# Half steps and a new list of steps in the attention stage of a hybrid decoder trunk

## The chip, the cores and the metric

The kernel runs on one core of one Trainium2 chip. The metric is device time in microseconds of one execution. TensorE (PE) multiplies, VectorE (DVE) and ScalarE (ACT) work on tiles in SBUF and on PSUM banks, GpSimd (POOL) does little here, and SyncE (SP) issues all loads.

## The reference

Two layers; each normalizes `x` (256 x 1024), projects it to 3100 columns, runs three groups of heads side by side, and ends with an MLP:

```python
for layer in range(DEPTH):                       # DEPTH = 2
    h = _rmsnorm(x, norm1_g[layer])
    proj = h @ w_in[layer]                       # 1024 x 3100
    o_a = _hgrn2(...)   # gated linear recurrence, 4 heads, state 64 x 64
    o_b = _nsa(...)     # 8 heads, 2 key groups: compressed + selected + window attention
    o_c = _fox(...)     # forgetting attention, 4 heads
    x = x + concat(o_a, o_b, o_c) @ w_o[layer]
    h2 = _rmsnorm(x, norm2_g[layer])
    x = x + square(relu(h2 @ w_up[layer])) @ w_down[layer]     # 1024 -> 4096 -> 1024
```

## The kernel before

All of it is one program without loops at run time. Weights come as 512 KB tiles of 128 x 1024 (`load`, tag `raw`, four slots). `load_split` (L223, L224) makes a high part `whi` on ACT and the rest `wlo` on DVE, and `mm3` (L229 to L231) multiplies three times, high by high, high by low, low by high. So every weight tile costs one long instruction on ACT, one on DVE and a run of products.

A layer has an attention stage and an MLP stage. In the attention stage, `proj_tok` and `proj_feat` make one of the projected chunks: "ag", "af", "ai", "aq" for the recurrence, "cmp" for the compressed keys and values, "kk", "q0", "q1" and "vg" for the sparse attention, "ck", "cq" and "cv" for the forgetting attention. A chunk is 48 products into one of two `acc` banks. "cv", "kk" and "q0" come first (`FIRST`).

The chains behind the chunks are these. The recurrence runs through seven levels `a_level` ("t0" to "t6"): a product of `Kc` and `Qbd` (L470), a masked copy of it (L479), and updates of `Qbd` and `Kc` on DVE (L485, L487) that the next level's product needs; `a_out` closes it. Keys and queries are normalized per head (`head_norm`), turned by four transposes (`head_transposes`, L560) and split again (`b_keys` L584, L585; `b_query` L595, L596; `c_query`, `c_keys`). The compressed keys take 16 small products per quarter (`b_compress`, "w0" to "w3", L613), whose weights `raw1` are used unsplit and hold `raw` slots till then, then `b_compressed` ("kc"): transposes, a GELU on DVE and ACT, a product that reads `hidT` (L640), a normalization, a transpose (L652) and the split into `KC` (L658, L659). `b_cmp_branch` ("cb0", "cb1") makes the compressed scores with `KC` (L772), a softmax, and transposes (L799). `head_b` ("b0" to "b7") and `head_c` ("c0" to "c3") make scores, softmax (L751 on DVE, L161 on ACT), scaling (L757 on ACT, L759 on DVE), transposes (L836, L841; L884) and a copy out of PSUM (L838, L843; L887); `pv_b` ("pb") and `pv_c` ("pc") multiply by the values (L850, L858; L895). "forget" prepares the decay. `wo_step` ("wo0" to "wo3") adds one weight tile each to the first column half of the output projection; the second half follows the list.

`ORDER` lists these steps; "+name" starts a chunk's projection, "name" does what follows it. The loop at the end of the stage calls them in that sequence. The sequence gives preference; the build then sorts the instructions of each engine and assigns slots, so the order on an engine need not be that of the list. PSUM has two `acc`, two `sc`, two `tr`, one `pa` and one `pv` bank. The list before:

```python
ORDER = ("+ag", "+af", "+cmp", "+aq", "kk", "af", "aq", "cmp", "t0", "+vg", "q0", "t1", "t2", "t3", "vg", "b2",
         "b1", "w0", "t4", "w1", "cv", "+ai", "w2", "w3", "ai", "t5", "kc", "b0", "+q1", "q1", "cb0", "t6", "b3",
         "cb1", "pb0", "forget", "a_out", "+ck", "+cq", "ck", "pb1", "cq", "b4", "b5", "b6", "c0", "pb2", "b7",
         "pb3", "c1", "wo0", "pc0", "wo1", "c3", "wo2", "c2", "pc1", "wo3")
```

Of the kernel before, what the change touches and what calls it, by code (L numbers as in the profile page):

```python
# [24 lines left out]
DH = 64  # L25
EPS = 1e-6
# [26 lines left out]
FIRST = ("cv", "kk", "q0")  # L53
ORDER = ("+ag", "+af", "+cmp", "+aq", "kk", "af", "aq", "cmp", "t0", "+vg", "q0", "t1", "t2", "t3", "vg", "b2",
# [3 lines left out]
WO_LAST = (0, 1, 2, 3)  # L58
# [77 lines left out]
def tile_block(ctx: ExitStack, tc: tile.TileContext, x_in, win, wo, wup, wdn, w1, vec, cst, out, dbg=None):  # L136
# [39 lines left out]
    def bank(tag):  # L176
        return T([P, 512], F32, tag, BANKS[tag], pp)
# [163 lines left out]
    for L in range(DEPTH):  # L341
# [149 lines left out]

        def a_out():
# [12 lines left out]
            V.tensor_copy(sd, psd[:, :8])  # L505
            po = bank("pa")
# [17 lines left out]
            V.tensor_mul(oA, oA, GA)  # L524
            ps = bank("pa")
# [50 lines left out]

        def b_keys(ps):

            ptr = head_transposes(head_norm(ps, 2, 4, 2, EPS, tabs["k"]), swap=(0,))
            for g in range(2):  # L580
# [7 lines left out]

        def b_query(c, ps):
            ptr = head_transposes(head_norm(ps, 2, 4, 1, DH * EPS, tabs["q"]))  # L590
            for a in range(2):
# [23 lines left out]

        def b_compressed():
            pre = pre_[0]
# [19 lines left out]
            V.reciprocal(u, u)  # L637
            V.tensor_mul(hidT[:, :, :, 0:NCMP], hx, u.rearrange("p (w g n) -> p w g n", w=2, g=2))
            pk = bank("sc")
            PE.matmul(pk[0:64, 0:64], hidT[:, 0].rearrange("p g n -> p (g n)"), vt[:, V_W2:V_W2 + 64], start=True, stop=True)  # L640
# [8 lines left out]
            V.tensor_sub(VC[64:80, :, 64:128], pvv, VC[0:16, :, 64:128].bitcast(F32))  # L649
            kcn = head_norm(pk[0:64, 0:64], 1, 1, 1.0 / DH, EPS, tbc, 64)  # L650
            pkt = bank("tr")
# [41 lines left out]

        def c_query(ps):
            ptr = head_transposes(head_norm(ps, 2, 4, 1, DH * EPS))
            for a in range(2):
# [5 lines left out]

        def c_keys(ps):
            ptr = head_transposes(head_norm(ps, 2, 4, 2, EPS))
            ckv = CK.rearrange("p (i a) t -> p a i t", a=2)
# [57 lines left out]
        def b_cmp_branch(g):  # L763

            ps = bank("sc")
            for j in range(4):
                hd = g * 4 + j
# [24 lines left out]
            A.activation(PCS[:, :, 64:80], pc, AF.Copy)  # L792
            V.tensor_sub(PCS[:, :, 32:48], pc, PCS[:, :, 0:16].bitcast(F32))
            pct = T([96, 4, S], F32R, "PCT", 2)
            for i in range(2):
# [13 lines left out]

        PT = {}  # L810

        def head_b(g, j):
# [18 lines left out]
            for i, (o, n) in enumerate(((0, P), (P, P), (256, 256), (512, 256))):  # L831
                scale(pt_[:, o:o + n], r[:, i:i + 1], i in SCALE_ACT)

            ps0 = bank("tr")
# [30 lines left out]
        def head_c(hd):  # L865
# [14 lines left out]
            for t, (o, n) in enumerate(((0, P), (P, 256))):  # L880
                scale(pt_[:, o:o + n], r[:, t:t + 1], t + 4 in SCALE_ACT)
            ps0 = bank("tr")
            for i in range(3):
# [60 lines left out]
        def wo_step(i):  # L944
# [8 lines left out]
            "ag": (proj_tok, None), "ai": (proj_tok, a_values), "af": (proj_feat, a_sigmoids), "aq": (proj_feat, a_query),  # L953
            "cmp": (proj_feat, b_cmp), "kk": (proj_tok, b_keys), "q0": (proj_tok, lambda ps: b_query(0, ps)),
            "q1": (proj_tok, lambda ps: b_query(1, ps)), "cq": (proj_tok, c_query), "ck": (proj_tok, c_keys),
            "cv": (proj_tok, c_values), "vg": (proj_vals, b_values),
        }
        step = {
            "t": a_level, "w": b_compress, "kc": b_compressed, "a_out": a_out,
            "cb": b_cmp_branch, "b": lambda i: head_b(i // 4, i % 4), "pb": lambda i: pv_b(i // 2, i % 2),  # L960
            "c": head_c, "pc": pv_c, "forget": c_forget, "wo": wo_step,
        }
# [164 lines left out]
```

## Time and profile before

| | us |
|---|---|
| median of three runs | 697.14 (696.44 to 698.15) |
| profiled execution, device time | 699.06 |
| its span, first to last instruction | 697.3 |
| attention stage of the first layer | from 29.5 to about 160.5 |
| attention stage of the second layer | from 371.8 to about 502.5 |
| TensorE busy | 675.9 |
| VectorE busy | 451.6 |
| ScalarE busy | 398.0 |

The stages overlap at their ends, so their bounds are rounded. A matmul's end is modelled, and products follow each other faster than one lasts; TensorE's idle time is therefore counted only when a gap outlasts the modelled end. PEclk 1.00 is the full clock, 2.4 GHz, and 0.50 is 1.2 GHz. In a timeline row the bracket gives the idle time of the engine ahead of the instruction and what ended it.

### The profile page before, as it was taken

How to read it: one execution, taken by the hardware profiler on the slowest of the kernel's cores; microseconds unless marked ns; L12 is line 12 of the kernel's file. 1: busy time of each engine (PE TensorE's matmuls, PEld its weight loads, DVE VectorE, ACT ScalarE, POOL GpSimd, SP SyncE). 2: the span in 40 equal slices, each digit the busy share in tenths (PEclk: the TensorE clock that was granted, in tenths of full speed). 3: DMA queues.
4: the chain of work that ended last, by engine and by line, in shares of the span. 5: the costliest groups of instructions: out<-in, count | busy, mean ns of one | idle time of the engine just before them, and what ended most of it. 6: DMA issues, size and time to landing. Idle time of an engine off the chain costs nothing.

```text
span 697.3 us, 11902 instructions
## 1 busy us (share of the span) xinstructions
PE 675.9 (97%) x4578; PEld 602.4 (86%) x4578; DVE 451.6 (65%) x987; ACT 398.0 (57%) x761; POOL 10.9 (2%) x28
## 2 busy tenths in 40 slices
PE   6999989999999999999999999899999999999997
PEld 5998979768988998899799988786799988998896
DVE  5878788838655545654587897786567456545552
ACT  7654675887444434554457556688865445444440
POOL 3100000000100000000000000000000000000000
PEclk9999998999999999999999999999999999999999
DMA  8852561206566666666546418421266666666631
GB/s 289 265 153 73 174 189 49 73 1 211 168 203 181 181 185 183 192 182 194 153 128 213 150 31 260 133 62 31 86 190 180 184 191 196 180 185 181 185 118 61
DMA packets 31017, 108.88 MB, mean 156 GB/s; under 512 B 3568, under 2 KB 4080, under 8 KB 30960
## 3 DMA queue, kind: packets, MB, share of 16 engines
q1 hardware_dynamic: 30960, 108.11, 51.5%
q8 instruction: 36, 0.59, 0.3%
q14 instruction: 21, 0.17, 0.1%
HBM read 107.05 MB, written 1.05 MB: 155 GB/s over the span
## 4 chain that ended last, share of the span: by engine, by line
PE 82%; DVE 8%; ACT 5%; DMA 3%; issue 1%; SPq 0%; ACTq 0%
PE sc L229 9%; PE sc L230 9%; PE sc L231 9%; PE acc L229 9%; PE acc L231 8%; PE acc L230 8%; PE pv L230 3%; PE pv L231 3%; PE pv L229 3%; DMA raw<-in_win_dram 3%; PE pa L231 3%; PE pa L230 3%; PE pa L229 3%; DVE wlo L224 2%; PE pv L858 2%; PE sc L613 1%
## 5 line engine op out<-in xcount | busy, mean ns | idle before, releaser
L224 DVE TENSOR_TENSOR wlo<-raw,whi 128x1024 fp32r<-128x1024 f32 (+2 forms) x197 | 235.2, 1197 | 139.1 <-PE sc L231 67.2
L223 ACT ACTIVATE whi<-raw 128x1024 fp32r<-128x1024 f32 (+2 forms) x197 | 204.3, 1041 | 195.1 <-PE sc L230 73.3
L229 PE MATMUL sc<-kt,whi 128*128 128x256 f32 x512 | 145.1, 283 | 0.0
L231 PE MATMUL sc<-kt,wlo 128*128 128x256 f32 x512 | 144.9, 283 | 0.0
L230 PE MATMUL sc<-kt,whi 128*128 128x256 f32 x512 | 144.8, 283 | 0.0
L229 PEld LDWEIGHTS sc<-kt,whi 128*128 128x128 f32 x512 | 98.0, 191 | 1.0 <-ACT s L1015 0.3
L230 PEld LDWEIGHTS sc<-kt,whi 128*128 128x128 f32 x512 | 98.1, 192 | 0.6
L231 PEld LDWEIGHTS sc<-kt,wlo 128*128 128x128 f32 x512 | 98.1, 192 | 0.0
L229 PE MATMUL acc<-whi,kt 128*128 128x256 f32 (+2 forms) x288 | 88.9, 309 | 2.7 <-ACT whi L223 2.7
L231 PE MATMUL acc<-whi,kt 128*128 128x256 f32 (+2 forms) x288 | 88.4, 309 | 0.2
L230 PE MATMUL acc<-wlo,kt 128*128 128x256 f32 (+2 forms) x288 | 87.4, 305 | 0.0
L229 PEld LDWEIGHTS acc<-whi,kt 128*128 128x128 f32 x288 | 56.8, 197 | 5.3 <-ACT whi L223 3.3
L231 PEld LDWEIGHTS acc<-whi,kt 128*128 128x128 f32 x288 | 56.3, 196 | 3.3 <-DVE kt L239 1.1
L230 PEld LDWEIGHTS acc<-wlo,kt 128*128 128x128 f32 x288 | 56.3, 196 | 1.5 <-DVE wlo L224 0.4
L229 PE MATMUL acc<-whi,big 128*128 128x512 f32 x128 | 50.7, 396 | 0.0
L230 PE MATMUL acc<-wlo,big 128*128 128x512 f32 x128 | 50.6, 395 | 0.0
L231 PE MATMUL acc<-whi,big 128*128 128x512 f32 x128 | 50.5, 394 | 0.0
L161 ACT ACTIVATE big<-big,nmx 128x128 f32<-128x128 f32 (+1 forms) x80 | 35.6, 447 | 16.4 <-DVE nmx L751 16.3
L1016 DVE TENSOR_TENSOR s<-s 128x512 f32<-128x512 f32 x32 | 22.0, 688 | 24.1 <-ACT s L1015 24.1
L751 DVE CUSTOM_DVE_ANT_0 big<-sc,cst 128x128 f32<-128x128 f32 (+1 forms) x80 | 26.5, 349 | 8.0 <-PE sc L876 4.2
L1015 ACT ACTIVATE s<-sc 128x512 f32<-128x512 f32 x32 | 18.8, 588 | 18.7 <-PE sc L231 18.7
L231 PEld LDWEIGHTS acc<-whi,big 128*128 128x128 f32 x128 | 24.1, 188 | 5.8
(299 smaller groups left out, 1183.3 us busy)
## 6 DMA issues: line engine op xcount, KB each, us to landing
raw<-in_wup_dram SPq DMA_DIRECT2D x64, 512.0 KB, 3.6
raw<-in_wdn_dram SPq DMA_DIRECT2D x64, 512.0 KB, 3.6
raw<-in_win_dram SPq DMA_DIRECT2D x44, 512.0 KB, 4.5
raw<-in_wo_dram SPq DMA_DIRECT2D x16, 512.0 KB, 3.9
raw<-in_w_dram SPq DMA_DIRECT2D x8, 512.0 KB, 3.6
raw<-in_win_dram SPq DMA_DIRECT2D x4, 426.0 KB, 3.7
out_dram<-x SPq DMA_DIRECT2D x4, 256.0 KB, 2.0
raw<-in_win_dram SPq DMA_DIRECT2D x2, 284.0 KB, 2.7
```

Source lines behind the costliest of these rows:

```text
L161: r = A.activation(*a, **k)
L223: A.activation(hi[:, c0], raw[:, c0], AF.Copy)
L224: V.tensor_sub(lo[:, c0], raw[:, c0], hi[:, c0].bitcast(F32))
L229: PE.matmul(ps, ah, wh, start=start, stop=False)
L230: PE.matmul(ps, ah, wl, start=False, stop=False)
L231: PE.matmul(ps, al, wh, start=False, stop=stop)
L613: PE.matmul(pre_[0][64 * w:64 * w + 35, 0:P], Z[:, w].rearrange("p g m -> p (g m)")[:, j:j + 273:8], raw1[w][:, c0:c0 + P], start=(j == 0) ...
L751: V.tensor_tensor_reduce(out=dst, in0=ps, in1=mask, scale=-1.0, scalar=3.0e38, op0=ALU.add, op1=ALU.min, accum_out=nmx)
L858: PE.matmul(po[64 * e_:64 * e_ + 64, t * P:S], VS[:, t, bi * 2 + g, :], PT[g * 4 + jj * 2 + e_][t][:, bi, :], start=False, stop=False)
L1015: A.activation(rl, pu[i], AF.Relu)
L1016: V.tensor_mul(rl, rl, rl)
```

## The change

Steps are cut in two or three at the point where one engine hands to another. `head_norm` is called by "kk", "q0", "q1", "ck" and "cq", and the transposes and splits of these become steps of their own, "/kk" and so on. `head_b` ends after the scaling, and its transposes become "h0" to "h7"; `head_c` is cut in the same place into "c" and "g", `b_cmp_branch` into "cb" and "ct", `a_out` into "ao0" to "ao2", and `b_compressed` into "kc0" to "kc2". The list of steps gets a new order with the new names. No instruction is added or dropped.

```diff
-ORDER = ("+ag", "+af", "+cmp", "+aq", "kk", "af", "aq", "cmp", "t0", "+vg", "q0", "t1", "t2", "t3", "vg", "b2",
-         "b1", "w0", "t4", "w1", "cv", "+ai", "w2", "w3", "ai", "t5", "kc", "b0", "+q1", "q1", "cb0", "t6", "b3",
-         "cb1", "pb0", "forget", "a_out", "+ck", "+cq", "ck", "pb1", "cq", "b4", "b5", "b6", "c0", "pb2", "b7",
-         "pb3", "c1", "wo0", "pc0", "wo1", "c3", "wo2", "c2", "pc1", "wo3")
+ORDER = ("kk", "+ag", "+af", "q0", "af", "+aq", "/kk", "/q0", "+cmp", "cmp", "aq", "t0", "+vg", "t1", "vg", "cv",
+         "b2", "t2", "b1", "h1", "t3", "w0", "w1", "+ai", "t4", "h2", "w2", "ai", "w3", "t5", "kc0", "kc1", "kc2",
+         "b0", "+q1", "t6", "q1", "h0", "cb0", "/q1", "ct0", "forget", "b3", "pb0", "ao0", "cb1", "h3", "pb1",
+         "+ck", "ao1", "+cq", "ck", "b4", "ct1", "cq", "b5", "h4", "/ck", "b6", "ao2", "h5", "/cq", "h6", "b7",
+         "wo1", "wo0", "h7", "c0", "c1", "g0", "g1", "pb2", "pb3", "c3", "wo2", "c2", "pc0", "g3", "g2", "pc1",
+         "wo3")
...
-        def b_keys(ps):
-
-            ptr = head_transposes(head_norm(ps, 2, 4, 2, EPS, tabs["k"]), swap=(0,))
+        def b_keys(xn):
+
+            ptr = head_transposes(xn, swap=(0,))
...
             for i, (o, n) in enumerate(((0, P), (P, P), (256, 256), (512, 256))):
                 scale(pt_[:, o:o + n], r[:, i:i + 1], i in SCALE_ACT)
+            PU[hd] = pt_
+
+        def head_bt(g, j):
+            hd = g * 4 + j
+            pt_ = PU.pop(hd)
 
             ps0 = bank("tr")
...
-            "cmp": (proj_feat, b_cmp), "kk": (proj_tok, b_keys), "q0": (proj_tok, lambda ps: b_query(0, ps)),
-            "q1": (proj_tok, lambda ps: b_query(1, ps)), "cq": (proj_tok, c_query), "ck": (proj_tok, c_keys),
+            "cmp": (proj_feat, b_cmp), "kk": (proj_tok, lambda ps: head_norm(ps, 2, 4, 2, EPS, tabs["k"])),
+            "q0": (proj_tok, lambda ps: head_norm(ps, 2, 4, 1, DH * EPS, tabs["q"])),
...
+        turn = {"kk": b_keys, "q0": lambda xn: b_query(0, xn), "q1": lambda xn: b_query(1, xn), "cq": c_query, "ck": c_keys}
+        normed = {}
...
+            elif name[0] == "/":
+                turn[name[1:]](normed[name[1:]])
             elif name in chunk:
-                chunk[name][1](ready[name])
+                normed[name] = chunk[name][1](ready[name])
```

## Rows read from the trace of the kernel before

**Rows 1.** The page: the span, and TensorE's busy time, share and instructions.
```profile
span 697.3 us, 11902 instructions
PE 675.9 (97%) x4578; PEld 602.4 (86%) x4578; DVE 451.6 (65%) x987; ACT 398.0 (57%) x761; POOL 10.9 (2%) x28
```

**Rows 2.** Windows by stage: start and end, length, each engine's busy time (instructions), clock.
```profile
core 0: us, PE busy (x) PEld busy (x) DVE busy (x) ACT busy (x) POOL busy (x), PEclk, DMA share, GB/s
29.49:52.60 23.11, 23.11 (x196) 23.11 (x195) 17.79 (x40) 13.04 (x20) 0.00 (x0) 1.00 0.59 185
52.60:160.50 107.90, 102.47 (x732) 85.73 (x731) 82.16 (x283) 76.59 (x206) 0.00 (x0) 0.97 0.30 94
160.50:371.80 211.30, 211.30 (x1367) 191.67 (x1366) 124.97 (x166) 108.94 (x153) 1.77 (x5) 1.00 0.62 183
371.80:502.50 130.70, 125.12 (x929) 108.16 (x928) 101.88 (x334) 89.78 (x227) 0.00 (x0) 0.99 0.36 111
```

**Rows 3.** TensorE's waits, 29.49 to 160.50 us: total, times, longest.
```profile
PE sc L640 <- DVE hidT L638: 1.2, 1, 1.2
PE pa L470 <- DVE m L487: 1.2, 2, 0.7
PE sc L772 <- DVE KC L659: 1.1, 1, 1.1
PE tr L841 <- ACT P L838: 0.7, 1, 0.7
```

**Rows 4.** TensorE's waits, 371.80 to 502.50 us; L772 and L841 have the same rows.
```profile
PE sc L640 <- DVE hidT L638: 1.5, 1, 1.5
PE pa L470 <- DVE m L487: 0.7, 1, 0.7
```

**Rows 5.** TensorE's timeline, 55 to 62 us: start, duration, instruction, idle time ahead.
```profile
55.68 1.15 PE L470 MATMUL pa<-Qbd,m 128*128 128x128 f32 x8
56.57 0.38 PE L229 MATMUL acc<-whi,kt 128*128 128x284 f32 x1
56.79 0.29 PE L230 MATMUL acc<-wlo,kt 128*128 128x284 f32 x1
56.92 0.29 PE L231 MATMUL acc<-whi,kt 128*128 128x284 f32 x1
...
60.56 0.60 PE L560 MATMUL tr<-cst,s 128*128 128x128 f32 x4
61.83 1.14 PE L470 MATMUL pa<-Qbd,m 128*128 128x128 f32 x8 [0.67 <-DVE m L487]
```

**Rows 6.** VectorE's timeline, 56 to 67 us: splits of the keys and queries.
```profile
59.62 0.76 DVE L585 SCALAR_TENSOR_TENSOR KLB<-tr,vec,KS 64x512 fp32r<-64x512 f32 x1
...
62.68 0.74 DVE L596 SCALAR_TENSOR_TENSOR qS<-tr,vec,qS 64x512 fp32r<-64x512 f32 x1
```

**Rows 7.** TensorE's timeline, 89 to 91 us: the product that reads `hidT`.
```profile
89.14 0.28 PE L229 MATMUL acc<-whi,kt 128*128 128x256 f32 x1
90.63 0.33 PE L640 MATMUL sc<-vec,hidT 128*64 128x64 f32 x2 [1.22 <-DVE hidT L638]
```

**Rows 8.** ScalarE's timeline, 86 to 88 us.
```profile
86.40 1.06 ACT L223 ACTIVATE whi<-raw 128x1024 fp32r<-128x1024 f32 x1 [1.58 <-DMA raw<-in_win_dram]
87.36 0.24 ACT L161 ACTIVATE gu<-gu 128x60 f32<-128x60 f32 x1
```

**Rows 9.** Waits of SP's queue, whole span: total, times, longest.
```profile
SPq L213 <- PE sc L613: 41.2, 4, 17.2
```

**Rows 10.** Windows in which the granted clock is low; columns as in rows 2.
```profile
104.80:111.65 6.85, 6.67 (x29) 6.39 (x30) 4.26 (x26) 2.02 (x7) 0.00 (x0) 0.50 0.27 77
449.56:452.98 3.42, 3.42 (x16) 3.14 (x16) 2.05 (x14) 1.85 (x7) 0.00 (x0) 0.50 0.13 53
```

**Rows 11.** Groups by line, whole span: busy, mean ns, idle ahead.
```profile
L161 ACT ACTIVATE big<-big,nmx 128x128 f32<-128x128 f32 (+1 forms) x80 | 35.6, 447 | 16.4 <-DVE nmx L751 16.3
L757 ACT ACTIVATE big<-big,rr 128x128 f32<-128x128 f32 (+1 forms) x48 | 18.8, 446 | 1.1 <-DVE rr L830 0.9
```

More of the change, by code (lines that the diff above doesn't have):

```diff
@@ L490, in a_level, with a_out0 @@
                 V.tensor_mul(th[0], tv[:, :, :, 0], tv[:, :, :, 1])
-        def a_out():
+        def a_out0():
             ps = bank("pa")
@@ L505, in a_out, with a_out1 @@
             V.tensor_copy(sd, psd[:, :8])
+            aos[:] = [AO, sd]
+        aos = []
+        def a_out1():
+            AO, sd = aos
             po = bank("pa")
@@ L524, in a_out, with a_out2 @@
             V.tensor_mul(oA, oA, GA)
+            aos[:] = [oA]
+        def a_out2():
+            oA = aos[0]
             ps = bank("pa")
@@ L587, in tile_block, with b_query @@
         qS = [T([P, 4, S], F32R, "qS", 2) for i in range(2)]
-        def b_query(c, ps):
-            ptr = head_transposes(head_norm(ps, 2, 4, 1, DH * EPS, tabs["q"]))
+        def b_query(c, xn):
+            ptr = head_transposes(xn)
             for a in range(2):
@@ L614, in b_compress, with b_compressed0 @@
                               raw1[w][:, c0:c0 + P], start=(j == 0), stop=(j == 15))
-        def b_compressed():
+        kst = {}
+        def b_compressed0():
             pre = pre_[0]
@@ L638, in b_compressed, with b_compressed1 @@
             V.tensor_mul(hidT[:, :, :, 0:NCMP], hx, u.rearrange("p (w g n) -> p w g n", w=2, g=2))
+        def b_compressed1():
             pk = bank("sc")
@@ L649, in b_compressed, with b_compressed2 @@
             V.tensor_sub(VC[64:80, :, 64:128], pvv, VC[0:16, :, 64:128].bitcast(F32))
-            kcn = head_norm(pk[0:64, 0:64], 1, 1, 1.0 / DH, EPS, tbc, 64)
+            kst["n"] = head_norm(pk[0:64, 0:64], 1, 1, 1.0 / DH, EPS, tbc, 64)
+        def b_compressed2():
+            kcn = kst["n"]
             pkt = bank("tr")
@@ L692, in tile_block, with c_query @@
         CC = T([P, S], F32R, "CC", 1)
-        def c_query(ps):
-            ptr = head_transposes(head_norm(ps, 2, 4, 1, DH * EPS))
+        def c_query(xn):
+            ptr = head_transposes(xn)
             for a in range(2):
@@ L701, in c_query, with c_keys @@
                 V.scalar_tensor_tensor(cqS[a][0:64], src, gcol, dh.bitcast(F32), ALU.mult, ALU.subtract)
-        def c_keys(ps):
-            ptr = head_transposes(head_norm(ps, 2, 4, 2, EPS))
+        def c_keys(xn):
+            ptr = head_transposes(xn)
             ckv = CK.rearrange("p (i a) t -> p a i t", a=2)
@@ L793, in b_cmp_branch, with b_cmp_t @@
             V.tensor_sub(PCS[:, :, 32:48], pc, PCS[:, :, 0:16].bitcast(F32))
+        def b_cmp_t(g):
             pct = T([96, 4, S], F32R, "PCT", 2)
@@ L806, in pv_evac @@
             evac_split(*kt_parts(mT, kt, ALL), po[:, 0:S])
-        PT = {}
+        PT, PU = {}, {}
         def head_b(g, j):
@@ L881, in head_c, with head_ct @@
                 scale(pt_[:, o:o + n], r[:, t:t + 1], t + 4 in SCALE_ACT)
+            PU[hd + 8] = pt_
+        def head_ct(hd):
+            pt_ = PU.pop(hd + 8)
             ps0 = bank("tr")
@@ L953, in tile_block @@
             "ag": (proj_tok, None), "ai": (proj_tok, a_values), "af": (proj_feat, a_sigmoids), "aq": (proj_feat, a_query),
-            "cmp": (proj_feat, b_cmp), "kk": (proj_tok, b_keys), "q0": (proj_tok, lambda ps: b_query(0, ps)),
-            "q1": (proj_tok, lambda ps: b_query(1, ps)), "cq": (proj_tok, c_query), "ck": (proj_tok, c_keys),
+            "cmp": (proj_feat, b_cmp), "kk": (proj_tok, lambda ps: head_norm(ps, 2, 4, 2, EPS, tabs["k"])),
+            "q0": (proj_tok, lambda ps: head_norm(ps, 2, 4, 1, DH * EPS, tabs["q"])),
+            "q1": (proj_tok, lambda ps: head_norm(ps, 2, 4, 1, DH * EPS, tabs["q"])),
+            "cq": (proj_tok, lambda ps: head_norm(ps, 2, 4, 1, DH * EPS)),
+            "ck": (proj_tok, lambda ps: head_norm(ps, 2, 4, 2, EPS)),
             "cv": (proj_tok, c_values), "vg": (proj_vals, b_values),
         }
+        turn = {"kk": b_keys, "q0": lambda xn: b_query(0, xn), "q1": lambda xn: b_query(1, xn), "cq": c_query, "ck": c_keys}
+        normed = {}
         step = {
-            "t": a_level, "w": b_compress, "kc": b_compressed, "a_out": a_out,
-            "cb": b_cmp_branch, "b": lambda i: head_b(i // 4, i % 4), "pb": lambda i: pv_b(i // 2, i % 2),
-            "c": head_c, "pc": pv_c, "forget": c_forget, "wo": wo_step,
+            "t": a_level, "w": b_compress, "kc": lambda i: (b_compressed0, b_compressed1, b_compressed2)[i](),
+            "ao": lambda i: (a_out0, a_out1, a_out2)[i](),
+            "cb": b_cmp_branch, "ct": b_cmp_t, "b": lambda i: head_b(i // 4, i % 4), "h": lambda i: head_bt(i // 4, i % 4),
+            "pb": lambda i: pv_b(i // 2, i % 2), "c": head_c, "g": head_ct, "pc": pv_c, "forget": c_forget, "wo": wo_step,
         }
```

## The prediction

> **What bounds the kernel now.** I read the page first, then the windows by stage, then TensorE's waits, then the stretches of time around the longest of them. By the page TensorE is busy 97% of the 697.3 us span, which looks like a full engine [rows 1]. The windows show where the missing part lies [rows 2]. Both MLP stages keep TensorE busy without a gap (211.30 of 211.30 us in the first layer), and so does the start of the attention stage, 23.11 of 23.11 us, in which the four projections "ag", "af", "cmp" and "aq" run end to end. All idle time that the change can reach lies after that: 107.90 - 102.47 = 5.43 us in the first layer, and 130.70 - 125.12 = 5.58 us in the second. VectorE and ScalarE are busy there for 82.16 and 76.59 of 107.90 us, so neither is the bound by its sum. What ends last is TensorE's own stream, and its holes are ends of chains: a product waits for VectorE or ScalarE to finish what an earlier product started [rows 3, 4].
>
> These brackets count too little. A product of 0.28 us is followed by the next after 0.12 us, so a wait also empties the pipeline. The "hidT" product starts 1.49 us after the product ahead of it instead of 0.12 us, a delay of 1.37 us, where the bracket says 1.22 us [rows 7]. I add 0.16 us (0.28 - 0.12) for each wait. With some 16 named waits in both layers the delay is 11.0 + 16 x 0.16 = 13.5 us.
>
> A second loss hides behind the first. After the waits near 101 to 105 us and 443 to 447 us the granted clock is 0.50, that is 1.2 GHz, for 6.85 us in the first layer and 3.42 us in the second [rows 10]. Ahead of the fall TensorE had stood idle several times in a row. At 2.4 GHz these 10.27 us would hold the same products in half the time, so at most 5.1 us is lost here.
>
> **The change, part by part.** No arithmetic goes and none comes: the same instructions on the same tiles, the same loads in nearly the same order on SP's queue ("cmp" and "aq" change places, and two wo tiles). The price is therefore all in what stands next to what. The list is an order of preference, not the engine's order: in the profile "t0" (L470) stands inside the "+vg" chunk, with 284-column products on both sides [rows 5]. So a half step helps only if, in its wait, some other product is ready that had no earlier use.
>
> *The k and q turns and "+cmp".* Today "t1" stands right behind the four transposes of "q0" and waits 0.67 us in the bracket, 61.83 - 60.56 - 0.44 = 0.83 us in starts [rows 5]. VectorE was late because it split a half of the turned keys for 0.76 us and later both halves of the queries, 0.74 us the first, between the updates of the levels [rows 6]. In the new list "/kk" and "/q0" stand ahead of "+cmp", whose 48 products last about 48 x 0.12 = 5.8 us. That chunk today runs in the 23.11 us stretch where nothing waits; after the change it covers the key and query splits and the "aq" work that opens the levels. The L470 waits are 1.2 us in the first layer and 0.7 us in the second, three waits, 2.4 us with the drains [rows 3, 4]. I take 2.0 us back: what stays is the gate work of "vg", still between the levels. Between 0 and 2.4.
>
> *The compressed-key chain.* L640, L772 and L841 idle 1.2, 1.1 and 0.7 us in the first layer; in the second L640 takes 1.5 us and the other two again 1.1 and 0.7 us [rows 3, 4]. With six drains that is 7.3 us. Why L640 is late can be read on ScalarE: the split of a weight tile waits 1.58 us for its transfer, and the small exponential of the chain (0.24 us) stands queued behind it [rows 8]. The transfer is late because SP's queue waited for weight slots that the compression products (L613) held: 41.2 us in four waits, 17.2 us the longest [rows 9]. In the new list kc0, kc1, kc2 still follow each other, so the cut alone gives this chain nothing. It gains only by what lies ahead of it: keys and queries are turned sooner, so b2 and b1 can give back the "sc" banks sooner, w0 and w1 run sooner, and the slots for the loads of "+q1" and "+ck" come free sooner. I take half, 3.6 us; the bounds are 0 and 7.3. The half-clock stretches come right behind these waits, so I take the same half of their 5.1 us, 2.5 us, with bounds 0 and 5.1.
>
> *The other cuts* (b/h, c/g, cb/ct, ao0 to ao2, the turns of q1, ck and cq). The rest of the delay, 13.5 - 2.4 - 7.3 = 3.8 us, is spread over waits of 0.2 to 0.4 us. Here transposes wait for scaled probabilities, which is the wait that b/h and c/g cut. I take 1.0 us, since each is short and the stream already mixes heads; between 0 and 3.8.
>
> *Switching.* A product of another kind costs more when the stream turns to it. The first 284-column product behind L470 takes 56.79 - 56.57 = 0.22 us, the next 56.92 - 56.79 = 0.13 us [rows 5], so one switch costs 0.09 us. The change cuts the TensorE work into 18 more pieces per layer (eight h, four g, two ct, two of ao, two of kc). At two more switches for each piece that would be 18 x 2 x 0.09 x 2 layers = 6.5 us. The other end is 0 or a little less, since a build that keeps chunks whole would save switches. I take 1.5 us, nearer to 0, because t0 shows that the stream is already mixed finer than the steps. The Trainium skill, "TensorE: Matmul & The Clock Gate", section "The mechanism", says that the reorder window pulls a weight load ahead of running matmuls when it goes to the background buffer. By that rule alone a switch would be free and the forecast 1.5 us lower; the 0.09 us in the row says it isn't free here.
>
> *Sum:* -2.0 - 3.6 - 2.5 - 1.0 + 1.5 = -7.6 us. The profiled execution took 699.06 us, 1.9 us over the median of 697.14; the sum gives 691.5 us against it and 689.5 us against the median.
>
> **The rivals.** *All waits go.* If the earlier start of the levels (5.8 us per layer) reaches everything behind it, the whole delay and the clock come back: 13.5 + 5.1 = 18.6 us, 678.5 us at most, with one switch term 680. For: 5.8 us per layer is about what each layer idles. Against: the kc chain has nothing new between its parts.
>
> *The waits move.* The list does not do what it says: the build already fills holes by itself, as t0 inside "+vg" shows, and the holes come where it judged a chain shorter than it is. Then new neighbours meet the same late chains, the three kc parts above all, and only the L470 waits go, against 1.5 us of switches: about 696.6 us, from 695.1 to 699.2. For: kc0 to kc2 unchanged and +ck, +cq still last. Against: the rows that name key and query work between the levels.
>
> *Slower: the tail lies bare.* All four FoX heads now come behind wo1 and wo0, with wo2, wo3 and the second column half of wo as their only cover. Each head has two exponentials at 447 ns and two scalings at 446 ns on ScalarE [rows 11], 1.8 us, so 7.1 us for four heads in a layer, in a stretch where products wait for them. If all of it lay bare it would cost 14.3 us in both layers; against the 7.6 us gained it decides from 3.8 us bare per layer. At three quarters bare, 10.7 us, less 7.6, the kernel takes 700.2 us; at all of it 703.8. For: products used as cover early are missing late, since their total is the same. Against: 72 products of 512 columns (wo2, wo3 and the four tiles of the second half) still stand between or behind these heads.
>
> **How the numbers follow.** Forecast (half of the chain's delay returned, 685 to 695 us): 0.50, predicted 689.5. All waits go (under 685): 0.12. The waits move (695.1 to 699.2): 0.18. Bare tail (over 699.2): 0.20. A measurement of this kernel can tell about 0.3%, 2.1 us, from no change. Faster by more than that is the first two cases, 0.62; within it 0.18; slower 0.20. The range from 682 to 701 us takes in the forecast and the moved waits, about half of the case in which all goes, and the near half of the bare tail: 0.50 + 0.18 + 0.06 + 0.09 = 0.83.
>
> **What would show it.** Right: no L470 wait on an update behind the transposes of q0; "+cmp" products between aq's work and t1; SP's waits on L613 well under 41.2 us; L640 and L772 under 0.6 us each; no or shorter stretches at 0.50 of the clock; attention windows of about 127 us instead of 131. Wrong: L640 and L772 as long as before (then the waits moved), or new idle time of TensorE in the last 25 us of each attention stage on transposes or pc products (then the tail is bare), or more switches at the same idle time.

## The result and the profile after

The changed kernel takes **679.32 us** (median of four runs, 678.19 to 680.39) where the kernel before took 697.12 beside it: a ratio of 0.974, 95% interval 0.9725 to 0.9754. It is 17.8 us faster. The forecast was 7.6 us, with 682 as the low end of the range: the sign was right, and the size was missed by more than half.

The page of the changed kernel, its span, busy times and the granted clock in 40 slices:

```profile
span 678.2 us, 11907 instructions
...
PE 662.6 (98%) x4578; PEld 598.6 (88%) x4578; DVE 451.2 (67%) x987; ACT 395.9 (58%) x761; POOL 11.6 (2%) x28
...
PEclk9999999999999999999999999999999999999999
```

Every engine runs as many instructions as before [rows 1]; TensorE has 13.3 us less of busy time, and no slice is under nine tenths of the full clock any more. The windows by stage (start and end, length, busy time of each engine, clock), from the transposes ahead of the list's first chunk on; the third and fourth are the rest of the first layer, its MLP, and the second attention stage:

```profile
29.26:52.37 23.11, 23.11 (x196) 23.11 (x195) 19.95 (x44) 16.90 (x26) 0.00 (x0) 1.00 0.64 203
52.37:159.09 106.72, 104.25 (x777) 90.72 (x776) 87.69 (x293) 78.87 (x213) 0.00 (x0) 1.00 0.34 109
159.09:361.08 201.99, 201.99 (x1322) 183.98 (x1321) 117.82 (x155) 102.11 (x141) 1.10 (x5) 1.00 0.62 183
361.08:491.64 130.56, 127.74 (x972) 113.92 (x970) 108.38 (x344) 95.14 (x239) 0.00 (x0) 1.00 0.39 123
```

They can't be laid beside rows 2 line by line, and that is a first finding. In rows 2 I ended the first attention stage at 160.50 us, where the idle time ends. By the first product of the MLP, before's stages run from 29.12 to 169.41 and from 371.47 to 510.67 us: 140.28 and 139.20 us. They now take 129.83 and 130.56 us. The MLP is as long as before (before 202.06 us, after 201.99), so the attention stages hold the whole gain: 10.45 + 8.64 = 19.1 us of the span. (Before's profiled run lay 1.9 us over its median and after's 0.6 us, hence 17.8 in the medians.)

TensorE's waits over the whole span of the changed kernel (total, times, longest):

```profile
PE tr L327 <- DMA cst<-in_cst_dram: 4.0, 1, 4.0
PE acc L231 <- ACT whi L225: 2.5, 1, 2.5
PE acc L231 <- DVE Z L587: 2.0, 2, 1.1
PE pa L472 <- DVE m L489: 1.5, 2, 0.8
PE sc L656 <- DVE hidT L652: 0.7, 1, 0.7
PE acc L231 <- DVE m L406: 0.3, 1, 0.3
PE sc L842 <- DVE nmx L770: 0.3, 1, 0.3
```

The lines have moved down: L640 is now L656, L772 is L791, L841 is L867, L470 is L472, L613 is L625. The first two rows are the start of the kernel, which the change does not touch. Of rows 3 and 4, the waits on KC and on P are gone, hidT is down to 0.7 us from 1.2 + 1.5, and the level waits on L472 are still there. The wait for Z, a tile that VectorE makes for the compressed keys out of the accumulator bank that a later chunk needs, is new.

**A loss that no row shows.** The rows of waits count only time in which TensorE has nothing in flight. A product's record lasts 0.28 us but the next can start after 0.12, so one that starts up to 0.16 us late leaves no idle time at all. I therefore took every product of the two attention stages and compared its distance to the next start with its pace in an undisturbed stretch (0.232 us for 512 columns, 0.130 for 284, 0.120 for 256, 0.110 below). The paces are chosen; both kernels run the same products, so a difference in the whole loss does not depend on them, while the level of the last part does. The excess falls into three parts: where the next product has idle time ahead of it (waits), where the clock is low, and the rest, late starts less early ones, without idle time (hidden). Both stages together, in us, rounded:

| kernel | time | ratio to before, 95% | waits | low clock | hidden | loss in all |
|---|---|---|---|---|---|---|
| before | 697.12 | 1 | 15.4 | 4.7 | 7.7 | 27.7 |
| after | 679.32 | 0.974 (0.9725 to 0.9754) | 7.5 | 0 | 1.1 | 8.6 |
| early_new | 687.05 | 0.9845 (0.983 to 0.986) | 11.4 | 1.6 | 3.4 | 16.5 |
| late_new | 685.32 | 0.9835 (0.9803 to 0.9866) | 9.0 | 1.8 | 3.9 | 14.7 |
| new_first | 693.65 | 0.9948 (0.9931 to 0.9964) | 19.9 | 4.6 | 0.0 | 24.5 |
| new_last | 712.84 | 1.0215 (1.0188 to 1.0242) | 27.1 | 13.6 | 1.8 | 42.5 |
| heads_whole | 687.13 | 0.9855 (0.9834 to 0.9875) | 11.6 | 1.5 | 3.9 | 17.0 |
| turns_whole | 696.33 | 0.9985 (0.9969 to 1.0002) | 18.3 | 8.7 | 0.0 | 27.0 |
| cbao_whole | 688.20 | 0.987 (0.9853 to 0.9888) | 14.0 | 0 | 3.0 | 16.9 |
| cmp_back | 679.77 | 0.9748 (0.973 to 0.9767) | 7.8 | 0 | 1.7 | 9.5 |
| pv_soon | 681.67 | 0.9768 (0.9745 to 0.979) | 9.3 | 0 | 1.6 | 10.8 |
| kq_early | 693.52 | 0.9932 (0.9905 to 0.9959) | 13.5 | 4.7 | 6.3 | 24.6 |
| late_turns_whole | 696.65 | 0.9983 (0.997 to 0.9995) | 17.6 | 7.7 | 0.0 | 25.3 |
| q1_whole | 694.03 | 0.9953 (0.9938 to 0.9967) | 17.0 | 5.9 | 0.7 | 23.6 |
| ckcq_whole | 689.65 | 0.9885 (0.9853 to 0.9918) | 15.4 | 3.0 | 0.7 | 19.0 |
| old_late_turns | 694.80 | 0.9962 (0.9946 to 0.9978) | 15.6 | 4.6 | 3.0 | 23.2 |
| tune2 | 677.52 | 0.9711 (0.9689 to 0.9734) | 5.8 | 0 | 1.3 | 7.1 |

The gain of 19.1 us is 7.9 of waits, 4.7 of the clock and 6.6 of hidden late starts, each rounded. For the last I had forecast a cost of 1.5. The other lines of the table are the experiments.

### The profile page after: what moved, and what is told of

The parts are those of the page before. It is cut to its first block, busy times and chain, and to the rows that moved or that the text cites. A ratio compares the mean times of both kernels' runs of the same rounds, so it can differ in the third digit from the quotient of the medians.

```text
span 678.2 us, 11907 instructions
## 1 busy us (share of the span) xinstructions
PE 662.6 (98%) x4578; PEld 598.6 (88%) x4578; DVE 451.2 (67%) x987; ACT 395.9 (58%) x761; POOL 11.6 (2%) x28
## 3 DMA queue, kind: packets, MB, share of 16 engines
HBM read 107.05 MB, written 1.05 MB: 159 GB/s over the span
## 4 chain that ended last, share of the span: by engine, by line
PE 83%; ACT 8%; DVE 4%; DMA 3%; issue 1%; SPq 0%; DVEq 0%
PE acc L231 9%; PE sc L231 9%; PE sc L232 9%; PE sc L233 9%; PE acc L232 9%; PE acc L233 9%; PE pv L232 3%; PE pv L231 3%; PE pv L233 3%; DMA raw<-in_win_dram 3%; PE pa L233 3%; PE pa L232 3%; PE pa L231 2%; ACT big L163 2%; PE pv L884 1%; DVE wlo L226 1%
## 5 line engine op out<-in xcount | busy, mean ns | idle before, releaser
L231 PE MATMUL acc<-whi,kt 128*128 128x256 f32 (+2 forms) x288 | 88.2, 306 | 4.6 <-ACT whi L225 2.5
L233 PE MATMUL acc<-whi,kt 128*128 128x256 f32 (+2 forms) x288 | 87.0, 303 | 0.0
L231 PEld LDWEIGHTS acc<-whi,kt 128*128 128x128 f32 x288 | 55.6, 193 | 8.0 <-ACT whi L225 3.1
L233 PEld LDWEIGHTS acc<-whi,kt 128*128 128x128 f32 x288 | 55.5, 193 | 1.4 <-DVE kt L237 0.3
L233 PEld LDWEIGHTS acc<-whi,big 128*128 128x128 f32 x128 | 24.1, 188 | 5.9
L231 PEld LDWEIGHTS acc<-whi,big 128*128 128x128 f32 x128 | 24.1, 188 | 5.2
```

The lines of the kernel that those rows point to most:

```text
L231: PE.matmul(ps, ah, wh, start=start, stop=False)
L233: PE.matmul(ps, al, wh, start=False, stop=stop)
```

## The experiments

Every kernel here is the changed one with another list, unless said otherwise; "whole" means that the half steps stand directly behind one another. The old list with all halves directly behind one another gives the program of before, instruction by instruction on every engine. So nothing was run for the cut alone: without the new order it is nothing.

### Which half of the list

early_new takes the new list up to "kc2" and the old one from there; late_new the reverse.

```diff
-"b0", "+q1", "t6", "q1", "h0", "cb0", "/q1", "ct0", "forget", "b3", "pb0", "ao0", ...
+"b0", "h0", "+q1", "q1", "/q1", "cb0", "ct0", "t6", "b3", "h3", "cb1", "ct1", "pb0", ...
```

> The new list up to kc2, then the old list with every step whole. Both lists have the same steps up to there, so the change divides cleanly. Theory A (the earlier start of the levels and keys lets the whole stage behind it fill up): at least two thirds of the 17.8 us, 683 to 687 us, and the stretches at half clock gone. Theory B (the gain is made behind kc, where the halves are spread): at most 5 us, 692 us or more, with the waits on KC (1.1 us) and on the copied probabilities (0.7 us) as before.

> The old list up to kc with every step whole, then the new list. Theory A: little, 692 us or more, and the wait on hidT (1.2 to 1.5 us) stays. Theory B: 681 to 686 us; hidT still late, but no wait on KC and no stretch at half clock. If the parts add, this saving and that of the other half make 17.8 us together.

Both halves are worth about as much: 0.9845 and 0.9835. The savings of loss, 11.2 and 13.0 us, add up to 24.2 where both together save 19.1, so part of the work is done by either. Neither account fits alone: early_new keeps one stretch at half clock and lies at the edge of the span given for an early gain, and yet has no wait on KC; late_new lies in the span given for a late gain, but keeps one such stretch too. The waits of SP's queue on the weight slots settle one point. Those of late_new are those of before [rows 9], those of the changed kernel are 6.8 us less:

```profile
SPq L215 <- PE sc L625: 41.2, 4, 17.2
```
```profile
SPq L215 <- PE sc L625: 34.4, 4, 11.6
```

late_new has the long slot wait and yet no wait on KC at all. Slots that come free sooner are not what ended that wait. Nor do they decide the wait on hidT: early_new has the short slot wait (34.4 us) and still waits 1.9 us on hidT.

### Order without the cut

new_first puts each step whole where its first half stands in the new list, new_last where its last half stands.

```diff
-"kk", "+ag", "+af", "q0", "af", "+aq", "/kk", "/q0", "+cmp", ...
+"kk", "/kk", "+ag", "+af", "q0", "/q0", "af", "+aq", "+cmp", ...
```
```diff
-"kk", "+ag", "+af", "q0", "af", "+aq", "/kk", "/q0", "+cmp", ...
+"+ag", "+af", "af", "+aq", "kk", "/kk", "q0", "/q0", "+cmp", ...
```

> The new order without the cuts: each step is whole again, at the place of its first half. The list with the cuts but the old order gives the same instructions in the same order on every engine as the kernel before, so the cut alone is worth nothing, and this run asks what the order alone is worth. Theory O (the order does it, since the build mixes within steps anyway): 679 to 683 us. Theory H (the room between the halves does it): 688 us or more, with waits of transposes on scaled probabilities.

> The new order without the cuts: each step is whole, at the place of its last part. Theory O: 679 to 683 us. Theory H: 688 us or more, here because scores and norms start late.

By its ratio new_first keeps 3.6 of the 17.8 us; new_last is 15 us slower than before. So the order alone, in the two placements tried, is worth little or harms, the cut alone is nothing, and the two together make the change. new_last is the bare chains that my slower rival feared, though not in the tail: its longest wait is at the head of the list, where a chunk needs the accumulator bank that the gate of "ag" (L406) still reads (total, times, longest):

```profile
PE acc L231 <- DVE m L406: 5.4, 2, 2.7
...
PE acc L231 <- DVE s L556: 2.2, 3, 1.1
PE tr L867 <- ACT P L864: 2.1, 4, 0.7
```

### Which family of halves

Three kernels keep the new list and make one family whole: the heads (h and g behind b and c), the turns of kk, q0, q1, ck, cq, or cb/ct and the three parts of a_out. A fourth moves "+cmp" back ahead of "+aq".

```diff
-"b4", "ct1", "cq", "b5", "h4", "/ck", "b6", "ao2", "h5", "/cq", "h6", "b7", "wo1", "wo0", "h7", "c0", "c1", "g0", "g1",
+"b4", "h4", "ct1", "cq", "b5", "h5", "/ck", "b6", "h6", "ao2", "/cq", "b7", "h7", "wo1", "wo0", "c0", "g0", "c1", "g1",
```
```diff
-"q1", "h0", "cb0", "/q1", "ct0", ... "ck", "b4", "ct1", "cq", "b5", "h4", "/ck", "b6", "ao2", "h5", "/cq",
+"q1", "/q1", "h0", "cb0", "ct0", ... "ck", "/ck", "b4", "ct1", "cq", "/cq", "b5", "h4", "b6", "ao2", "h5",
```
```diff
-"cb0", "/q1", "ct0", "forget", "b3", "pb0", "ao0", "cb1", "h3", "pb1", "+ck", "ao1", ...
+"cb0", "ct0", "/q1", "forget", "b3", "pb0", "ao0", "ao1", "ao2", "cb1", "ct1", "h3", "pb1", "+ck", ...
```
```diff
-"af", "+aq", "/kk", "/q0", "+cmp", "cmp", "aq",
+"af", "+cmp", "+aq", "/kk", "/q0", "cmp", "aq",
```

> The new list with only the twelve heads whole again (each h right behind its b, each g behind its c); all other cuts stay. With all cuts undone at the place of the first half the kernel took 693.7 us, 14.3 more than with them. Theory H1 (the room between a head's scores and its transposes carries the gain): 688 to 692 us, with transposes that wait for ScalarE's scaling (L776) or copy (L864) again. Theory H2 (other cuts carry it): under 683 us.

> The new list with only the five turns of keys and queries right behind their norms; all other cuts stay. Theory T1 (the room between norm and turn matters most): 686 us or more, with L572 waiting for the norm (L564). Theory T2: under 682 us.

> The new list with the compressed branches and the recurrence's output whole again (ct behind cb, ao1 and ao2 behind ao0). In the changed kernel 24 products of ao1 lie where the kernel before waited for KC. Theory K1 (they are what fills that hole): the waits on KC or on the copied probabilities come back, 1.1 and 0.7 us in each layer, and a stretch at half clock; 684 to 689 us. Theory K2 (the hole had closed already by what comes ahead): under 682 us.

> The new list with one step moved back: +cmp ahead of +aq, as in the list before, so that nothing but the transposes stands between aq's projection and the levels. Theory C1 (the prediction: these 48 products give the chains 5.8 us of cover, and with it most of the gain): 687 us or more, with a wait on Qbd or a level's update ahead of t0 and t1. Theory C2 (the levels wait for VectorE anyway): 679 to 682 us, with less wait of vg's products for the bank that Z frees.

The turns carry most: without their cut the ratio is 0.9985, the gain is lost. Heads cost 7.8 us, a little less than the span for heads that carry the gain, and the transposes wait 1.4 us for ScalarE's copy (L864) again; cb/ct and a_out cost 8.9 us. The three sum to 33.7 us, against 14.3 when all are whole at once (new_first), so these prices do not add. TensorE's waits of turns_whole:

```profile
PE sc L791 <- DVE KC L678: 2.1, 2, 1.1
PE tr L572 <- DVE s L564: 1.9, 2, 1.2
...
PE acc L231 <- DVE s L556: 1.5, 2, 1.1
PE sc L842 <- DVE nmx L770: 1.3, 5, 0.4
```

The wait on KC of rows 3 is back, and the transposes of the turns (L572) now wait for their norm. In cbao_whole the time lies where I put it if the chain waits came back, but they did not: it has new waits of 2.0 us on L556 and 1.0 us on ScalarE's split of `kt` instead. And "+cmp" is worth nothing where it now stands: 679.77 against 679.32. It only trades one wait for another (no wait for Z, but more on the levels):

```profile
PE pa L472 <- DVE m L489: 2.8, 4, 1.0
```

### What a switch between two kinds of product costs

> The changed kernel with 512 added products per... two sets per layer at the head of the list, on operands that are long ready, with a result that nobody reads: 32 transposes in a piece, 32 products of 256 columns in a piece, then eight times four transposes and four products; first with 128 output partitions, then with 64 as the pv products have. Added work, the same output. What it measures is the price of a turn between two kinds with no wait possible. Theory S (the short losses that the change took, some 4.3 us less in 44 fewer late starts, are turns of the stream): the mixed part takes longer than the two whole pieces by 15 turns of about 0.09 us, 1.3 us for each set, and more with 64 partitions, up to 0.19 us a turn, 2.8 us. Rival H (they are short waits on other engines, too short to show as idle, since each product's record lasts 0.28 us and the next starts after 0.12): the mixed part takes within 0.3 us of the pieces, under 0.02 us a turn. In between, the price times the number of turns says how much of the 25.87 us of before and 21.61 us of after is either.

```diff
+        def price():
+            hi = [kt_parts(hT, k, ALL)[0] for k in range(2)]
+
+            def tr_(d, n):
+                for i in range(n):
+                    PE.transpose(d[:, (i % 2) * P:(i % 2 + 1) * P], ident, ident)
+
+            def mm_(d, n, w):
+                for i in range(n):
+                    PE.matmul(d[0:w, 256:512], hi[i % 2][:, 0:w], hi[1 - i % 2], start=True, stop=True)
+
+            for w in (P, 64):
+                d = bank("tr")
+                tr_(d, 32)
+                mm_(d, 32, w)
+                for _ in range(8):
+                    tr_(d, 4)
+                    mm_(d, 4, w)
```

The windows of the first layer: two pieces with 128 output partitions, the same mixed, then both with 64 partitions:

```profile
28.58:35.90 7.32, 7.32 (x66) 7.32 (x65) 6.34 (x25) 2.54 (x7) 0.00 (x0) 1.00 0.61 208
35.90:43.17 7.27, 7.27 (x67) 7.27 (x65) 0.00 (x0) 0.00 (x0) 0.00 (x0) 1.00 0.00 0
43.17:50.32 7.15, 7.15 (x67) 7.15 (x65) 0.00 (x0) 0.00 (x0) 0.00 (x0) 1.00 0.01 2
50.32:57.57 7.25, 7.25 (x67) 7.25 (x66) 0.00 (x0) 0.00 (x0) 0.00 (x0) 1.00 0.00 0
```

Fourteen more switches change 7.32 to 7.27 us, and 7.15 to 7.25: from -0.004 to +0.007 us a switch; the second layer shows the same to 0.01 us. For these two pairs, with operands that are ready, a switch costs nothing. The 0.09 us that I read in rows 5 is there in this run too, but it only moves: behind transposes the four products take 0.56 us where four inside a piece take 0.48, and the four transposes ahead of them take 0.35 where four inside a piece take 0.43. I had counted the late start and not the early one.

The test leaves out the products that matter, though. Its 64-partition products all write the same half. Those of `pv_b` write the lower and the upper 64 output partitions alternately, and side by side two of them can start 0.01 us apart. In one piece they are fast, in several slow. TensorE's timeline before shows four pieces and what follows each:

```profile
141.22 0.65 PE L858 MATMUL pv<-P,VS 128*64 128x256 f32 x4
141.80 0.33 PE L836 MATMUL tr<-cst,big 128*128 128x128 f32 x1
142.06 0.65 PE L858 MATMUL pv<-P,VS 128*64 128x128 f32 x4
142.64 0.33 PE L836 MATMUL tr<-cst,big 128*128 128x128 f32 x1
...
143.01 0.86 PE L858 MATMUL pv<-P,VS 128*64 128x256 f32 x6
143.80 0.39 PE L850 MATMUL pv<-PCT,VC 96*128 96x256 f32 x1
...
145.44 0.65 PE L858 MATMUL pv<-P,VS 128*64 128x256 f32 x2
146.01 0.39 PE L874 MATMUL sc<-CK,m 128*128 128x256 f32 x1
```

and after, the same number and sizes in one piece:

```profile
111.63 1.52 PE L884 MATMUL pv<-P,VS 128*64 128x256 f32 x16
113.08 0.39 PE L876 MATMUL pv<-PCT,VC 96*128 96x256 f32 x1
```

From the start of a piece to the next kind, the sixteen take 1.45 us in one piece and 0.58 + 0.58 + 0.79 + 0.57 = 2.52 us in four, 0.36 us for each further piece, without idle time. These are not waits: a piece of two takes 0.57 or 0.58 us at all eight places where it stands in the two kernels, and so does a piece of four at its eight places. (The order inside a piece counts too: in the tail of the changed kernel sixteen in another order take 1.79 us.) In both stages together the `pv_b` products stand in 20 pieces before and 12 after, 16.3 and 13.7 us. The compression products (L613, now L625), which write two halves as well, stand in 8 and 4 pieces, 8.7 and 7.6 us. That is 3.7 of the 6.6 us of hidden gain. Over the 17 kernels of the table `pv_b` goes the same way: with 10 pieces these products, with the start into each piece, are 0.5 us ahead of their pace, with 20 they are 4.3 us behind it. What the other 2.9 us are is not shown.

### Small moves

pv_soon moves pb2 behind h5 and pb3 behind h7. kq_early is the old list with the first step of the prediction alone.

```diff
-"h5", "/cq", "h6", "b7", "wo1", "wo0", "h7", "c0", "c1", "g0", "g1", "pb2", "pb3", "c3",
+"h5", "pb2", "/cq", "h6", "b7", "wo1", "wo0", "h7", "pb3", "c0", "c1", "g0", "g1", "c3",
```
```diff
-"+ag", "+af", "+cmp", "+aq", "kk", "af", "aq", "cmp", "t0", "+vg", "q0", "t1",
+"+ag", "+af", "+cmp", "+aq", "kk", "/kk", "q0", "/q0", "af", "aq", "cmp", "t0", "+vg", "t1",
```

> The new list with pb2 and pb3 alone moved forward, each right behind the half step of its last head (pb2 behind h5, pb3 behind h7), so that their 64-partition products meet heads that are still in work, as in the old list; nothing else. Theory S (part of the gain is that these products now run in one piece behind a wait-free stretch): the late part of the stage loses 1 to 3 us in both layers again, the kernel is 680.5 to 683, with no new wait over 1 us. Theory W (the gain there is cover: the pb products filled holes of c0, c1, g0 and g1): new waits of transposes on scaled probabilities, 2 us or more, 682 to 686 us. Null: their place makes no difference, 679 to 680.

> The old list, every step whole, with one change: kk and its turn, q0 and its turn stand right behind the fourth projection, ahead of the work of af, aq and cmp. This is the prediction's first step by itself. The prediction: the level waits on L470 go, 2.0 us, and keys and queries ready sooner also help the compressed-key chain: 691 to 695 us. Rival: as in the changed kernel the level waits stay near 1.5 us, since the levels wait for VectorE's own chain and not for the splits, and the keys and queries ready sooner are worth nothing by themselves: 695 to 698 us. Against the early part of the new list alone, which gave 10.8 us, it says how much of that is this step.

pv_soon costs 2.3 us, in the span that I gave for broken-up pv products; but its loss grows by 1.7 us in waits and only 0.5 hidden (14 pieces of `pv_b` instead of 12). So most of what it loses is cover, and the broken-up products are the smaller part. kq_early gains 4.6 us, as forecast for that step with the chain behind it. But the L472 waits, which it was to end, are longer than before (2.1 + 0.8 + 0.2 = 3.1 us against 2.3). The wait on KC is gone and that on hidT is 1.6 instead of 2.7 us: the gain of the early turns comes out in the compressed-key chain, not in the levels.

### The late turns

late_turns_whole makes the turns of q1, ck and cq whole, q1_whole and ckcq_whole one part of it (shown: q1). old_late_turns is the old list with these three half steps moved a few steps behind their norms.

```diff
-"+q1", "t6", "q1", "h0", "cb0", "/q1", "ct0",
+"+q1", "t6", "q1", "/q1", "h0", "cb0", "ct0",
```

> The new list with the turns of q1, ck and cq right behind their norms, kk and q0 still in halves. With all five turns whole the gain was lost, 696.3 us. If the three late turns carry it (their transposes then wait for ScalarE and VectorE in the stretch where the half-clock stretches came back, from 100 us on): 690 to 696 us, a KC wait and half-clock stretches again. If the two early ones carry it (all five norms' waits at the head of the list, 1.9 us on L572): 680 to 684 us, no half clock. The two together cost 17 us; the waits that came back (18.3 against 7.5 us, half clock 8.7 us) lie mostly behind 100 us, so I expect the first.

> The new list with the turn of q1 alone right behind its norm; the turns of ck and cq stay in halves. With the three late turns whole the kernel lost the whole gain, 17.3 us. In its trace the first loss stands where q1 is: KC's second half on VectorE queued behind a product of a_out that stood on TensorE behind the waiting transposes, a KC wait of 1.05 us in each layer, and the half-clock stretch behind 104 us. Theory Q (a wait early in the dense part starts it, and the rest follows from it): 688 to 696 us, KC waits and a half-clock stretch in the first layer. Rival T (ck and cq in the tail carry it, where each of their transposes waits for a norm): under 684 us, at most the two KC waits, no half clock.

> The other part: the turns of ck and cq right behind their norms, that of q1 in halves. Theory Q: under 684 us, since up to 105 us it is the changed kernel. Rival T: 688 to 696 us, with waits of L572 and of L842 on nmx behind 118 us as with all three. If neither part costs more than 5 us and both together 17, the losses feed each other, and the half clock is where.

> The old list with one change: the turns of q1, ck and cq stand two or three steps behind their norms (behind cb0, b4 and b5), all else whole and in the old place. In the new list these three half steps carry 17.3 us. If they are enough by themselves: 680 to 686 us. If they are needed but not enough, since in the old list the waits of the compressed-key chain (3 us of brackets in each layer) come ahead of them and stay: 690 to 697 us, with L656, L791 and L867 waiting as before and fewer waits behind 110 us.

The three late turns alone lose the whole gain (696.65). Each part loses more than half of it by itself: q1 14.7 us, ck and cq 10.3 us, together 17.3. Neither of my two accounts foresaw that both would. In the old list the same three half steps gain 2.5 us: needed, not enough, and its KC wait stays (2.3 us).

What q1's turn does can be followed product by product. TensorE's timeline of the changed kernel (start, duration, instruction, idle time ahead):

```profile
97.17 0.59 PE L521 MATMUL pa<-m,AT 128*128 128x64 f32 x4
97.69 0.24 PE L671 MATMUL tr<-cst,s 64*64 64x64 f32 x1
97.87 0.66 PE L862 MATMUL tr<-cst,big 128*128 128x128 f32 x4
98.36 0.56 PE L521 MATMUL pa<-m,AT 128*128 128x64 f32 x4
...
99.87 0.39 PE L867 MATMUL tr<-cst,big 128*128 128x128 f32 x2
100.09 0.33 PE L521 MATMUL pa<-m,AT 128*128 128x64 f32 x2
...
100.68 1.04 PE L791 MATMUL sc<-KC,qS 128*128 128x32 f32 x8
101.58 0.68 PE L757 MATMUL sc<-cst,LF 128*128 128x256 f32 x2
```

and of q1_whole:

```profile
97.26 0.24 PE L671 MATMUL tr<-cst,s 64*64 64x64 f32 x1
97.44 0.66 PE L521 MATMUL pa<-m,AT 128*128 128x64 f32 x4
...
99.49 0.39 PE L521 MATMUL pa<-m,AT 128*128 128x64 f32 x2
100.93 1.76 PE L791 MATMUL sc<-KC,qS 128*128 128x32 f32 x8 [1.05 <-DVE KC L678]
102.53 1.20 PE L757 MATMUL sc<-cst,LF 128*128 128x256 f32 x2
```

The first product with KC (L791) waits for a chain that begins at the transpose L671: scaled copies on ScalarE and VectorE. It starts 3.0 us behind the transpose in the changed kernel, 3.7 in q1_whole. In the changed kernel the transposes of head 0 (L862, L867) lie in that gap beside a_out's products. In q1_whole they stand behind the turn of q1 in the list, which waits for its norm, and come 9.6 us later (107.50 us); so TensorE runs dry at 99.9. VectorE's queue adds the rest:

```profile
99.92 0.69 DVE L525 TENSOR_TENSOR sA<-sA,pa 128x512 f32<-128x512 f32 x1 [1.20 <-PE pa L521]
100.64 0.24 DVE L678 SCALAR_TENSOR_TENSOR KC<-tr,vec,KC 64x30 fp32r<-64x30 f32 x1
```

The second half of KC stands behind a step of a_out that waits for TensorE's last product. More is lost right behind it; columns of the window as above:

```profile
101.10:107.93 6.83, 6.65 (x29) 6.17 (x30) 5.35 (x21) 1.34 (x5) 0.00 (x0) 0.50 0.26 77
```

Right behind the wait the granted clock is 0.50, 1.2 GHz, for 6.83 us: a product of 256 columns starts each 0.21 us instead of 0.12. Such a stretch stands in before at nearly the same place [rows 10], and none in the changed kernel. That the wait brings the low clock is not shown by this alone: cbao_whole has 14.0 us of waits and no such stretch. Of the 15.0 us by which q1_whole loses more than the changed kernel, the two KC waits are 2.1 and the clock 5.9; the rest is mostly other waits, the longest sum (2.3 us) on a split by ScalarE (L240).

### A try at what is left

```diff
-"+aq", "/kk", "/q0", "+cmp", "cmp", "aq", "t0", "+vg", "t1",
+"+aq", "/kk", "+cmp", "cmp", "aq", "/q0", "t0", "+vg", "t1",
```

> An attempt on what the changed kernel has left: the turn of q0 behind cmp and aq instead of ahead of +cmp, so that VectorE makes Z 1.5 us sooner (the two splits of the queries, 0.74 and 0.76 us, no longer stand ahead of it) and the second bank of +vg no longer waits for Z (1.1 and 1.3 us in starts). If that is all: 677 us. If the queries' splits now stand in the levels, as in the kernel before, the L472 waits grow by as much: 679 to 680 us. Slower than 681 only if b2 and b1 then wait for the queries.

```profile
PE pa L472 <- DVE m L489: 1.5, 2, 0.8
PE sc L842 <- DVE nmx L770: 0.8, 1, 0.8
PE acc L231 <- DVE Z L587: 0.6, 1, 0.6
```

The wait for Z falls from 2.0 to 0.6 us, the level waits do not grow, and the kernel takes 677.52 us (676.65 to 678.07), below every run of the changed one. The two were not run side by side, and their ratios to before have intervals that overlap (0.9689 to 0.9734, 0.9725 to 0.9754), so the 1.8 us are likely rather than sure. The mechanism is the one expected.

## Why the prediction was wrong

**The bound.** Right: TensorE's own stream, with holes at the ends of chains. But the loss was put at 13.5 us of delay and 5.1 of clock, 18.6 us. It was 27.7: 15.4 in waits, 4.7 of clock, and 7.7 that no wait and no window shows as idle. The stage was cut off too early as well, at the last idle time. The nine microseconds behind it are attention work, but no loss: they run 0.1 us ahead of their pace. The hidden loss of the first layer lies between 112 and 160.5 us, 4.0 us, where all pieces of `pv_b` stand.

**Switching, +1.5 us: the step that failed.** I counted 18 more pieces per layer in the list and gave them a price. On the engine there are fewer pieces, not more: in both attention stages TensorE switches from one line's products to another's 360 times instead of 378 (the three lines of a split product counted as one), `pv_b` stands in 12 pieces instead of 20, and the compression products in 4 instead of 8. Late starts of 0.03 us or more, outside waits and low clock, fell from 282 to 238, and the hidden part from 7.7 to 1.1 us. That is a gain of 6.6 where I had a cost of 1.5, 8.1 us of the difference of 11.5 between the forecast of -7.6 and the span's -19.1; 3.7 of it is shown to be pieces. The price was wrong as well: the 0.09 us were one late start without the early one beside it. In the run price a switch of ready products costs -0.004 to +0.007 us, while a further piece of `pv_b` costs 0.36 us. The rule that I weighed here, that a weight load is pulled ahead of running products ("TensorE: Matmul & The Clock Gate", section "The mechanism", in the Trainium skill), was set aside for the row. The run agrees with what I drew from it, a free switch, for the two pairs measured; the pieces of `pv_b` do not. By that rule the forecast would have been 1.5 us lower, still 10 us short of the span's change; that the change makes fewer pieces was in neither.

**The clock, -2.5 us: mis-sized.** All of it went, 4.7 us. I took the half of it because I took the half of the chain. It does not follow the waits in proportion: late_new, with 9.0 us of waits left, still has 1.8 us of it, and cbao_whole, with 14.0, has none. What decides it is open.

**The compressed-key chain, -3.6 us: size too small, reason not borne out.** Its three brackets (hidT, KC, P) were 2.7, 2.3 and 1.4 us in both layers; 0.7 is left, so 5.7 went. I had said that the cut of kc gives nothing because kc0 to kc2 follow each other in the list, and that a gain must come through weight slots. The list is not the engine's order: a_out and head 0 lie between the transpose and the KC product in the timeline above. And late_new closes the wait on KC with slots as late as before, while early_new, with slots as early as after, keeps 1.9 us on hidT.

**The k and q turns, -2.0 us: wrong place.** The level waits were to go; they are 1.5 us instead of 1.9. The 48 products of "+cmp" cover nothing that the place before did not (cmp_back), and the two banks that "+vg" needs met the wait for Z, which the trace of before does not have. The early turns are worth 4.6 us all the same (kq_early), out of the chain.

**The other cuts, -1.0 us.** All waits fell by 7.9 us where the three steps had 6.6 together; this part of the sum was nearly right, but partly by luck. In the new order these cuts do more than close old waits: without the three late turns the kernel has 17.6 us of waits, more than the 15.4 of before, and loses the whole gain. The sum had no term for waits that the new order brings and the cuts keep away.

**The rivals.** "All waits go" (0.12) had the time, 678.5 to 680, but by luck: it reached it by an earlier start of the levels, which cmp_back denies, and without the hidden part; 7.5 us of waits are still there. "The waits move" came true in one place, Z. The bare tail did not come: behind 100 us of the stage's work the changed kernel loses 1.3 and 1.4 us in the two layers where before lost 3.9 in each, and no wait there exceeds 0.07 us. That the 72 products named against this rival are the cover was not tested.

**The signs to look for.** L791 waits no more and L656 0.7 and 0.15 us, as said for "right"; the clock, as said; SP's waits 34.4, hardly "well under" 41.2; the windows 129.8 and 130.6 us, but measured to the right end, from 140.

What stays open: what the other 2.9 us of the hidden gain are, why the build makes fewer pieces of the new list, and what decides where the clock falls.

## What to carry to other kernels

Measure the loss of a full engine as its length less its undisturbed pace, product by product; the idle brackets showed 11.0 of 27.7 us here. A cut of a chain is worth nothing without an order that puts ready work into the gap, and the order little without the cut; what one such gap costs depends on the others, so test them together and don't add up single prices. The list is only a preference: look in the engine's timeline for what really lies between the halves, and in how many pieces products stand that start in pairs.

## What was not expected of the hardware

Products that write the lower and the upper half of the output partitions alternately can start two at a time, 0.01 us apart: sixteen in one piece take 1.45 us, two by themselves 0.58 us, and neither shows idle time. Mixing transposes with products of 256 columns that all write the same partitions is free when the operands are ready (7.27 us mixed, 7.32 in pieces; 7.25 and 7.15 with 64 output partitions), though single starts shift by up to 0.1 us. And a short wait can stand right ahead of a long stretch at the low clock: in q1_whole 1.05 us ahead of 6.83 us at 1.2 GHz. The attention stages of new_last lose 13.6 us to that clock, while those of cbao_whole, with 14.0 us of waits, have no such stretch.
